# Expert weights of a mixture-of-experts block: 16 KB buffers and runs in place of 8 KB ones

## The chip, the cores and the metric

The kernel runs on one core of a Trainium2 chip. A core has a matrix engine (TensorE, PE in the rows; PEld is its weight load), a vector engine (VectorE, DVE), an activation engine (ScalarE, ACT), GpSimd (POOL) and a sync engine (SyncE, SP), which issues nearly all transfers here. Transfers go from the chip's memory (HBM) to the on-chip memory (SBUF, 128 partitions) by 16 DMA engines. The metric is the time of one execution in device microseconds (us); lower is better.

## The reference, cut to what matters

One transformer block over 256 latent tokens of width 1024 with 256 context tokens. A token mixer (projections, a gated linear recurrence, a spatial MLP, an output projection) is followed by a mixture of 32 experts, of which each token uses 4:

```python
x = x + g1 * token_mix(p_lat, s_fwd, s_bwd, ...)
x = x + g2 * moe_ffn(modulate(x, norm2_g, sh2, sc2), ...)
return rms_norm(x, final_g)

def expert_block(xblk, e):                       # w1: (32, 1024, 2048), w2: (32, 1024, 1024), float32
    z = xblk @ w1[e] + b1[e]
    gate = minimum(z[:, :1024], 7); lin = clip(z[:, 1024:], -7, 7)
    return (gate * sigmoid(1.702 * gate) * (lin + 1)) @ w2[e] + b2[e]
```

Every expert's weights are read once: 8 MB of `w1` and 4 MB of `w2` each, 384 MB in all (1 MB is 1024 KB here). The values stay float32.

## The kernel before

**The mixer.** Its weights come in granules of 256 columns: 1 MB, 128 partitions by 8 rows of 256 values, so that one contiguous run is 1 KB (`Granule`, load at L293). A granule is split into a high and a low part (`ghi` on ScalarE, `glo` on VectorE, L241 and L242), in two halves, and multiplied at L321. After the attention come, in this order: section 6 of `w_in` (4 granules, into `v`), section 5 (4, into `u`, with the small products `o_ps` at L624), `w_branch_b` (4), section 7 and `w_branch_a` (8), `w_out` (4), and then the routing.

**The experts.** `w1_step` (L795 to L800) loads 128 rows of `w1` (1 MB, L797): one row of 2048 values, 8 KB, to a partition, then multiplies 64 gathered tokens by it. Eight such steps make one expert's first product; `swiglu` and `turned` (L818) follow. `w2_steps` (L823 to L839) loads `w2` in four pieces of 1 MB (L832): 16 KB of it belong to a partition, taken in two runs of 8 KB. The second product of an expert comes after the first product of the next one. `scatter` (L855) adds the result to the tokens.

**The end.** For the last expert `last_columns` (L857 to L880) takes `w2` in four blocks of 256 columns, each in two transfers of 512 KB (L863, runs of 1 KB). A block is multiplied (L868), scaled (L871), scattered (L876, L877) and multiplied by the final norm's weight (L880); after the last block come the norm's factor and the output.

**Buffers.** `wtile` (L45) takes the next name from the list `slots`: 8 KB to a partition each. During the attention there are three (`ring`); for the loads after the third granule of section 6 there are seven more (`ringb`, in the space that the attention leaves). For the experts `d0` to `d3`, `big1` (once) and five of `ringc` are added: 20 buffers, 20 MB.

**What sets the order.** A scheduler decides the order on each engine ahead of the run by its own model of the times; in the expert part TensorE keeps the order of the program (`manual_schedule`). Each engine takes its instructions in order. A transfer is issued when its buffer is free and one of eight semaphores that stand for transfers under way is free.

Of the kernel before, what the change touches and what calls it, by code (L numbers as in the profile page):

```python
# [16 lines left out]
P = 128  # L17
# [14 lines left out]
def kernel(  # L32
# [10 lines left out]
    slots = [(ring, "w")] * RING_A  # L43

    def wtile(shape):  # L45

        pool, tag = slots.pop(0)
        if tag != "big1":
            slots.append((pool, tag))
        return pool.tile(shape, F32, name="w", tag=tag)  # L50

# [155 lines left out]
    def mod_col(j, h, res):  # L207
        a, step = mod_sums(j, h)

        def finish():  # L210
            step(1)
            pt = bank("tp", (P, 4, 2))
            for k in range(4):
                te.matmul(pt[:, k], a[:, k * P:(k + 1) * P], ones[:, 0:2], start=True, stop=True)
            ve.tensor_add(res[:, 4 * h:4 * h + 4], pt[:, :, 0], bmcol[:, 8 * j + 4 * h:8 * j + 4 * h + 4])
        return [lambda: step(0), finish]
# [134 lines left out]

    pack2 = pack_rows("pack2", [(rows(norm2_g), 8), (rows(lb_fwd), 16), (rows(lb_bwd), 16), (rows(gnorm_g), 1), (b_s[0], 8)])
    cols2 = unpack(pack2, "cols2")
    n2col, gncol = cols2[:, 0:8], cols2[:, 40:41]
# [179 lines left out]
    for j in range(5):  # L534
# [22 lines left out]
        if j == 0:  # L557
# [11 lines left out]
            nc.sync.dma_start(wr_sb, w_router[0].rearrange("(k p) e -> p k e", p=P))  # L569
# [20 lines left out]
    def more_slots(n):  # L590
        if n == LATER:
            slots.extend([(ringb, "w")] * RING_B)

    more_slots(0)
# [4 lines left out]
    for j in range(4):  # L599
        pp = two(win(6, j), hT[0], True)  # L600
        more_slots(j + 1)
        sc.activation(v[:, :, j * 256:(j + 1) * 256], pp, AF.Gelu)
# [13 lines left out]
    for j in range(4):  # L616
        pp = two(win(5, j), hT[0], False)
        more_slots(j + 5)
# [54 lines left out]
    for j in range(4):  # L673
# [14 lines left out]
        for k in range(2):  # L688
            for tt in range(2):
                te.transpose(pt[:, k, tt * P:(tt + 1) * P], acc[:, tt, (2 * j + k) * P:(2 * j + k + 1) * P], ident)  # L690
# [56 lines left out]
    slots[4:4] = [(consts, f"d{i}") for i in range(4)] + [(consts, "big1")]  # L747
    slots += [(ringc, "w")] * RING_C
# [46 lines left out]
    def w1_step(zz, xT, kt, src):  # L795
        w = wtile([P, 2 * D])
        nc.sync.dma_start(w, src)  # L797
        for n in range(2):
            for h in range(2):
                te.matmul(zz[n][h * C:(h + 1) * C], xT[:, kt], w[:, n * D + h * 512:n * D + (h + 1) * 512],  # L800
# [22 lines left out]
    def w2_steps(hT2, selb, w2e):  # L823
# [6 lines left out]
        for k2 in range(4):  # L830
            w = wtile([P, 2, D])
            nc.sync.dma_start(w, w2e[:, k2 // 2, k2 % 2 * 2:k2 % 2 * 2 + 2])  # L832
# [9 lines left out]
    def scatter(y, pT, wcol, old=None, tts=(0, 1)):  # L842
# [6 lines left out]
        for tt in tts:  # L849
            pcs = [bank2(f"sc{h}") for h in range(2)]  # L850
# [6 lines left out]
    def last_columns(j, hT2, pT, selb, wcol, w2e):  # L857

        selb = selb.to_broadcast([96, C])
        s = slice(j * 256, (j + 1) * 256)  # L860
        w = wtile([P, KT, 256])
        for h in range(2):
            nc.sync.dma_start(w[:, 4 * h:4 * h + 4], w2e[:, h, :, s])  # L863
        py = bank2(("py", "misc")[j % 2], (P, 256))
        te.matmul(py[0:C], selb, b3[:, 2, s], start=True, stop=False, skip_group_check=True)
        for kt in range(KT):
            h = kt % 2
            te.matmul(py[h * C:(h + 1) * C], hT2[:, kt % 4, (kt // 4) * C:(kt // 4) * C + C], w[:, kt],  # L868
                      start=kt == 1, stop=kt >= KT - 2, skip_group_check=True)
        y = wk.tile([P, 256], F32, name="y")  # L870
        ve.tensor_mul(y, py, g2bc[:, s])  # L871

        def rest():
            for tt in range(2):
                pc = bank2((("sc0", "sc1"), ("gate", "lin"))[j % 2][tt], (P, 256))
                te.matmul(pc, pT[:, tt * P:(tt + 1) * P], y, start=True, stop=True)  # L876
                ve.scalar_tensor_tensor(acc[:, tt, s], pc, wcol[tt], acc[:, tt, s], op0=OP.mult, op1=OP.add)  # L877
                junk = wk.tile([P, 256], F32, name="junk", tag="g", bufs=1)
                sc.activation(junk, acc[:, tt, s], AF.Square, accum_out=ss8[:, tt, j:j + 1])
                (gp if j < 3 else ve).tensor_mul(accg[:, tt, s], acc[:, tt, s], fgbc[:, s])  # L880
        return rest
# [21 lines left out]
    w1e = lambda e, kt: w1[0, e, kt * P:(kt + 1) * P]  # L903
# [4 lines left out]
    with tc.manual_schedule(engines={mybir.EngineType.PE}):  # L908
# [3 lines left out]
        for e in range(E):  # L912
# [8 lines left out]
            if e == E - 1:  # L921
                slots[:] = [x for x in slots if x[1] not in ("d0", "d1")]
                bc = consts.tile([P, 2, D], F32, name="bc", tag="d0")
# [3 lines left out]
                ss8 = consts.tile([P, 2, 4], F32, name="ss8")  # L927
            zz = w1_open(sel(e)) if e else first_zz
            for kt in range(KT):
                w1_step(zz, xTs[e], kt, w1e(e, kt))  # L930
# [20 lines left out]
        rest = last_columns(0, hT2, pT, sel(e), wcols(e), w2e(e))  # L951
        scatter(*ready[1:])
        for j in range(1, 4):
            then = last_columns(j, hT2, pT, sel(e), wcols(e), w2e(e))
            rest()
            rest = then
        rest()

    most = nc.values_load(maxc[0:1, 0:1], min_val=0, max_val=T)
    with tc.If(most > C):  # L960
# [5 lines left out]
        with tc.For_i(0, E, 1) as er:  # L966
# [10 lines left out]
            for blk in range(1, T // C):  # L977
# [9 lines left out]
                for kt in range(KT):  # L987
                    w1_step(zz, xT, kt, w1[0, bass.ds(er, 1), kt * P:(kt + 1) * P].rearrange("a p n -> (a p) n"))
# [60 lines left out]
```

## Time and profile before

| | us |
|---|---|
| median of three runs | 1451.89 (1451.4 to 1457.05) |
| the profiled execution | 1452.21 |
| its span, first to last instruction | 1450.4 |
| TensorE busy, share of the span | 93% |
| hardware DMA queue, share of 16 engines' span | 84.3% |

A matrix product counts as busy from when it starts until its modelled end, also where products overlap, so that 93% is not TensorE at its peak. Times within the execution are us from the span's start. "SPq" is the sync engine's issue of a transfer. In a row of the sequence of instructions, rows of one kind are merged (x8 is eight in a row) and the duration is from the first one's start to the last one's end. One float32 product is two matrix instructions in the rows.

### The profile page before, as it was taken

The page shows a single profiled execution, that of the slowest core. Times are in us where ns is not written, and L with a number is a line of the kernel's source. Part 1 is how long each engine was busy: PE and PEld are TensorE (multiplying, and loading weights), DVE is VectorE, ACT ScalarE, POOL GpSimd, SP SyncE. Part 2 cuts the span into 40 slices and gives each one's busy share as a digit, 9 for nine tenths or more (in the row PEclk, how much of TensorE's full clock was granted, in tenths as well). Part 3 has the DMA queues.
Part 4 walks back from the last instruction along what each step waited for, and adds up shares of the span by engine and source line. Part 5 has one row for each costly group of instructions (what it writes and reads, how often), then busy time and mean ns, then how long its engine had stood idle before and what let it go on. Part 6 is the DMA issues. An engine that isn't in the chain of part 4 may idle for free. (4 is left out here: it accounts for less than half of the span.)

```text
span 1450.4 us, 19638 instructions
## 1 busy us (share of the span) xinstructions
PE 1345.7 (93%) x8218; PEld 743.0 (51%) x8218; DVE 640.0 (44%) x1108; ACT 307.9 (21%) x497; POOL 161.1 (11%) x109
## 2 busy tenths in 40 slices
PE   6979798979999999999999999999999999899996
PEld 4979787878999843333333332323323233232323
DVE  5498888887768613222222322222222222222223
ACT  2463354454444310100000000100001000010001
POOL 3054323240064000000000000000000000000001
PEclk8999999999999999999999999999999999999999
DMA  9536252534995899999999999999999999999994
GB/s 333 188 116 204 88 195 67 201 120 162 292 295 220 312 388 414 420 420 421 421 420 420 420 421 420 421 420 421 421 420 421 420 421 422 420 420 421 420 419 173
DMA packets 130751, 487.43 MB, mean 336 GB/s; under 512 B 9161, under 2 KB 71746, under 8 KB 82018
## 3 DMA queue, kind: packets, MB, share of 16 engines
q1 hardware_dynamic: 129810, 483.37, 84.3%
q0 software_dynamic: 848, 2.75, 0.6%
q8 instruction: 66, 1.08, 0.3%
q14 instruction: 27, 0.22, 0.0%
HBM read 485.04 MB, written 1.05 MB: 335 GB/s over the span
## 5 line engine op out<-in xcount | busy, mean ns | idle before, releaser
L800 PE MATMUL gate<-w,xT 128*64 128x512 f32 x1024 | 270.4, 606 | 18.6 <-DMA w<-in_w_dram 17.2
L800 PE MATMUL lin<-w,xT 128*64 128x512 f32 x1024 | 263.5, 592 | 0.0
L836 PE MATMUL py<-w,hT 128*64 128x512 f32 x992 | 228.1, 597 | 20.8 <-DMA w<-in_w_dram 20.8
L321 PE MATMUL acc<-hh,ghi 128*128 128x256 f32 x576 | 166.9, 290 | 12.1 <-ACT iv L394 12.1
L855 DVE SCALAR_TENSOR_TENSOR acc<-sc,wts,acc 128x512 f32<-128x512 f32 x124 | 87.4, 746 | 205.3 <-PE sc L852 205.3
L321 PE MATMUL acc<-hh,glo 128*128 128x256 f32 x576 | 165.5, 288 | 11.3 <-DVE glo L242 11.3
L321 PE MATMUL acc<-hl,ghi 128*128 128x256 f32 x576 | 165.1, 287 | 0.0
L242 DVE TENSOR_TENSOR glo<-w,ghi 128x1024 fp32r<-128x1024 f32 (+1 forms) x99 | 139.1, 1409 | 50.2 <-ACT ghi L241 49.8
L836 PEld LDWEIGHTS py<-w,hT 128*64 128x64 f32 x992 | 66.3, 136 | 162.8 <-issue 98.6
L800 PEld LDWEIGHTS lin<-w,xT 128*64 128x64 f32 x1024 | 74.3, 137 | 145.5 <-issue 145.5
L800 PEld LDWEIGHTS gate<-w,xT 128*64 128x64 f32 x1024 | 61.0, 136 | 163.6 <-issue 96.6
L241 ACT ACTIVATE ghi<-w 128x1024 fp32r<-128x1024 f32 (+1 forms) x102 | 102.4, 1007 | 144.3 <-PE acc L321 106.6
L321 PEld LDWEIGHTS acc<-hh,ghi 128*128 128x128 f32 x576 | 111.4, 194 | 13.3 <-ACT iv L394 12.5
L321 PEld LDWEIGHTS acc<-hh,glo 128*128 128x128 f32 x576 | 111.3, 193 | 13.0 <-DVE glo L242 12.8
L321 PEld LDWEIGHTS acc<-hl,ghi 128*128 128x128 f32 x576 | 111.4, 193 | 0.7 <-issue 0.7
L839 DVE TENSOR_TENSOR y<-py,g2h 128x512 f32<-128x512 f32 x31 | 21.4, 691 | 188.1 <-PE py L836 188.1
L925 POOL DMA_DIRECT2D bc<-in_final_g_dram x1 | 0.6, 557 | 934.3 <-DMA w<-in_w_dram 934.3
L773 ACT ACTIVATE xT<-misc,sh,a 128x128 f32<-128x128 f32 (+1 forms) x68 | 30.7, 451 | 272.4 <-DVE xT L775 272.4
L807 DVE TENSOR_SCALAR g<-gate 128x512 f32<-128x512 f32 x32 | 22.1, 691 | 147.1 <-PE gate L800 147.1
L321 PE MATMUL acc<-ghi,hh 128*128 128x256 f32 x256 | 73.3, 288 | 14.0 <-DVE og L383 6.4
L775 DVE TENSOR_SCALAR xT<-misc,a,sh 128x128 f32<-128x128 f32 (+1 forms) x68 | 27.2, 401 | 131.0 <-PE misc L769 120.5
L808 ACT ACTIVATE s<-g 128x512 f32<-128x512 f32 x32 | 20.2, 630 | 292.5 <-DVE g L807 292.5
(316 smaller groups left out, 1732.4 us busy)
## 6 DMA issues: line engine op xcount, KB each, us to landing
w<-in_w_dram SPq DMA_DIRECT2D x380, 1024.0 KB, 19.8
w<-in_w_in_dram SPq DMA_DIRECT2D x33, 1024.0 KB, 5.6
w<-in_w_mod_dram SPq DMA_DIRECT2D x24, 1024.0 KB, 6.6
w<-in_w_branch_a_dram SPq DMA_DIRECT2D x4, 1024.0 KB, 16.2
w<-in_w_branch_b_dram SPq DMA_DIRECT2D x4, 1024.0 KB, 12.2
w<-in_w_out_dram SPq DMA_DIRECT2D x4, 1024.0 KB
w<-in_w_dram SPq DMA_DIRECT2D x8, 512.0 KB, 8.7
w<-in_w_in_dram SPq DMA_DIRECT2D x12, 256.0 KB, 7.5
```

The costliest lines, as they stand in the source:

```text
L241: sc.activation(hi, src, AF.Copy)
L242: eng.tensor_sub(lo, src, hi)
L321: te.matmul(o, l, r, start=opens and kt == 0 and n == 0, stop=kt == KT - 1 and n == 2, skip_group_check=True)
L773: sc.activation(xT[:, kt], pg[:, k], AF.Identity, bias=sh2[:, kt:kt + 1], scale=a2[:, kt:kt + 1])
L775: ve.tensor_scalar(xT[:, kt], pg[:, k], a2[:, kt:kt + 1], sh2[:, kt:kt + 1], op0=OP.mult, op1=OP.add)
L800: te.matmul(zz[n][h * C:(h + 1) * C], xT[:, kt], w[:, n * D + h * 512:n * D + (h + 1) * 512], start=False, stop=kt == KT - 1, skip_group_c ...
L807: ve.tensor_scalar(g, zz[0], 7.0, None, op0=OP.min)
L808: sc.activation(s, g, AF.Sigmoid, scale=1.702)
L836: te.matmul(py[h * C:(h + 1) * C], hT2[:, kt % 4, (kt // 4) * C:(kt // 4) * C + C], w[:, k, h * 512:(h + 1) * 512], start=False, stop=kt = ...
L839: ve.tensor_mul(y, py, g2h)
L855: ve.scalar_tensor_tensor(acc[:, tt, s], pcs[h], wcol[tt], old[:, tt, s], op0=OP.mult, op1=OP.add)
L925: gp.dma_start(fgbc, bcast(final_g, D))
```

## The change

- Buffers have a size of one unit (8 KB to a partition) or two (16 KB). `ringb` is three buffers of two units (was seven of one) and `ringc` three of two (was five of one); `ring`, `d0` to `d3` and `big1` stay. That is 20 MB as before. `ringb` no longer serves the mixer, which keeps the three of `ring` to its end.
- `two_units` loads two units of expert weights: into a buffer of two units with one transfer of 2 MB and runs of 16 KB, or, where the next buffer is of one unit, with two transfers of 1 MB and runs of 8 KB. For that a partition holds two neighbouring rows of `w1`; the order of the tokens' columns follows (`cols3`, `view(..., [[2, P]])`, the router's weights in four transfers, three small loads `pack3`).
- The last expert's `w2` comes in four transfers of 1 MB (`last_columns`): half the rows by 512 columns, runs of 2 KB. The last half is multiplied in two blocks of 256 columns. The `scatter` before it uses four PSUM banks in place of two.
- In the expert part SyncE keeps the order of the program too.

```diff
-    slots = [(ring, "w")] * RING_A
+    slots = [(ring, "w", 1)] * RING_A
+    def wtile(shape, units=1):
+        i = next(i for i, s in enumerate(slots) if s[2] == units)
+        pool, tag, _ = slots.pop(i)
+        if tag != "big1":
+            slots.append((pool, tag, units))
+        return pool.tile(shape, F32, name="w", tag=tag)
+    def two_units(src, n):
+        r = 4096 // n
+        if slots[0][2] == 2:
+            w = wtile([P, r, n], 2)
+            nc.sync.dma_start(w, src)
+            return w[:, :r // 2], w[:, r // 2:]
+        ws = [wtile([P, r // 2, n]) for _ in range(2)]
+        for i, w in enumerate(ws):
+            nc.sync.dma_start(w, src[:, i * (r // 2):(i + 1) * (r // 2)])
+        return ws
...
-                te.matmul(pt[:, k], a[:, k * P:(k + 1) * P], ones[:, 0:2], start=True, stop=True)
+                te.matmul(pt[:, k], view(a, k // 2 * 256 + k % 2, [[2, P]]), ones[:, 0:2], start=True, stop=True)
...
+    pack3 = late.tile([12, 256], F32, name="pack3")
+    for i, src in enumerate((norm2_g[0], b_mod[0, 3 * D:4 * D], b_mod[0, 4 * D:5 * D])):
+        nc.sync.dma_start(pack3[4 * i:4 * i + 4], src.rearrange("(r f) -> r f", f=256))
...
-            nc.sync.dma_start(wr_sb, w_router[0].rearrange("(k p) e -> p k e", p=P))
+            for r in range(4):
+                nc.sync.dma_start(wr_sb[:, 2 * r:2 * r + 2], w_router[0, r * 256:r * 256 + 256].rearrange("(p k) e -> p k e", k=2))
...
-    def more_slots(n):
-        if n == LATER:
-            slots.extend([(ringb, "w")] * RING_B)
...
-    slots[4:4] = [(consts, f"d{i}") for i in range(4)] + [(consts, "big1")]
-    slots += [(ringc, "w")] * RING_C
+    slots[:] = ([(ringb, "w", 2)] * RING_B + slots + [(consts, f"d{i}", 1) for i in range(4)] + [(consts, "big1", 1)] +
+                [(ringc, "w", 2)] * RING_C)
...
-                    te.matmul(pg[:, k], x1[:, tt, kt * P:(kt + 1) * P], tok[:, tt], start=tt == 0, stop=tt == 1)
+                    te.matmul(pg[:, k], view(x1, tt * D + kt // 2 * 256 + kt % 2, [[2, P]]), tok[:, tt], start=tt == 0, stop=tt == 1)
...
-    def last_columns(j, hT2, pT, selb, wcol, w2e):
+    def last_columns(c, hT2, pT, selb, wcol, w2e):
...
+        def products(u):
...
+            w = wtile([P, 4, 512])
+            nc.sync.dma_start(w, w2e[:, u, :, c * 512:(c + 1) * 512])
+            for b in blocks if u else [slice(0, 512)]:
...
-    with tc.manual_schedule(engines={mybir.EngineType.PE}):
+    with tc.manual_schedule(engines={mybir.EngineType.PE, mybir.EngineType.SP}):
...
+        first, last = (last_columns(c, hT2, pT, sel(e), wcols(e), w2e(e)) for c in range(2))
+        first[0]()
+        scatter(*ready[1:], banks=("sc0", "sc1", "gate", "lin"))
+        first[1]()
+        last[0]()
+        first[2]()
+        last[1]()
+        last[2]()
...
-RING_B = 7
-RING_C = 5
+RING_B = 3
+RING_C = 3
```

What the sync engine issues from the last loads of the attention part on, before (128x8x256 is a mixer granule of 1 MB, x6 is six of them; `in_w_dram` is an expert weight):

```order
L188 DMA w<-in_w_mod_dram 128x4x512
L293 DMA w<-in_w_in_dram 128x8x256 x6
L293 DMA w<-in_w_branch_a_dram 128x8x256
L293 DMA w<-in_w_in_dram 128x8x256 x2
L293 DMA w<-in_w_branch_b_dram 128x8x256 x4
```

And now, at the same place of the same engine:

```order
L201 DMA w<-in_w_mod_dram 128x4x512
L306 DMA w<-in_w_in_dram 128x8x256 x7
L58 DMA w<-in_w_dram 128x4096 x3
L306 DMA w<-in_w_in_dram 128x8x256
L306 DMA w<-in_w_branch_b_dram 128x8x256 x4
```

Three expert transfers of 2 MB have moved ahead of the last granule of section 5. At the end of the mixer the same engine had, before (the eight and four are one expert's `w1` and `w2`; `maxc` is the read of the largest expert's count):

```order
L293 DMA w<-in_w_out_dram 128x8x256 x4
L797 DMA w<-in_w_dram 128x2048 x16
L832 DMA w<-in_w_dram 128x2048 x4
L959 TENSOR_LOAD maxc
L959 ISA x2
L797 DMA w<-in_w_dram 128x2048 x8
```

And now:

```order
L306 DMA w<-in_w_out_dram 128x8x256 x4
L62 DMA w<-in_w_dram 128x2048 x8
L58 DMA w<-in_w_dram 128x4096 x3
L986 TENSOR_LOAD maxc
L986 ISA x2
L58 DMA w<-in_w_dram 128x4096 x3
L62 DMA w<-in_w_dram 128x2048 x8
L58 DMA w<-in_w_dram 128x4096 x6
```

From there eight transfers of 1 MB and six of 2 MB alternate to the end: 114 of 2 MB in all, 152 of 1 MB and the last four. The order of the expert weights was that of their use before as well.

TensorE's order where the last granule of section 5 begins, before (`acc_4127` is the third granule's result, `acc_4198` the last one's; the small products of the third and fourth part of `u` stood inside and behind the last granule):

```order
L321 MATMUL acc_4127<-hl0_169,ghi_4156 128x256
L321 MATMUL acc_4127<-hh0_168,glo_4157 128x256
L321 MATMUL acc_4198<-hh0_168,ghi_4199 128x256
L321 MATMUL acc_4198<-hl0_169,ghi_4199 128x256
L321 MATMUL acc_4198<-hh0_168,glo_4200 128x256
```

And now, at the same place (`o_ps` is the small products, `ub` a part of the router's offset, `acc_4210` the last granule's result):

```order
L334 MATMUL acc_4139<-hh0_168,glo_4169 128x256
L671 MATMUL ub_4550<-wr_sb_61,sh2_71 128x32 x3
L640 MATMUL o_ps_4198<-wsT_987,v_3725 128x128 x4
L640 MATMUL o_ps_4269<-wsT_987,v_3725 128x128 x4
L334 MATMUL acc_4210<-hh0_168,ghi_4211 128x256
```

Small products that don't need the last granule now stand ahead of it. TensorE's order in the last expert's last columns, before:

```order
L865 LDWEIGHTS sel_69
L865 MATMUL misc<-b_4507,sel_69 64x256
L868 MATMUL misc<-w,hT_9605 64x256 x8
L876 MATMUL sc_9707<-y,pT 128x256
L876 MATMUL sc_9713<-y,pT 128x256
L876 MATMUL gate<-y,pT 128x256
L876 MATMUL lin<-y,pT 128x256
```

And now:

```order
L882 LDWEIGHTS sel_69
L882 MATMUL misc<-b_4519,sel_69 64x512
L888 MATMUL misc<-w,hT_9389 64x512 x4
L899 MATMUL sc_9432<-y,pT 128x512
L899 MATMUL sc_9438<-y,pT 128x512
L888 MATMUL misc<-w,hT_9389 64x256 x8
L899 MATMUL gate<-y,pT 128x256
L899 MATMUL lin<-y,pT 128x256
L899 MATMUL sc_9468<-y,pT 128x256
L899 MATMUL sc_9474<-y,pT 128x256
```

The four blocks of 256 columns have become one of 512 and two of 256, over the same columns and rows in all.

## Rows read from the trace of the kernel before

**Rows 1.** Stretches: us, busy us of PE PEld DVE ACT POOL, clock, DMA share, GB/s.

```profile
380.00:410.00 30.00, 30.00 (x258) 30.00 (x257) 21.00 (x34) 13.09 (x17) 3.50 (x6) 1.00 1.09 344
436.00:510.00 74.00, 72.92 (x597) 68.21 (x598) 51.78 (x91) 31.66 (x51) 16.31 (x11) 1.00 0.72 274
510.00:560.00 50.00, 47.88 (x255) 20.56 (x251) 10.82 (x26) 7.18 (x13) 0.00 (x0) 1.00 0.98 391
560.00:1400.00 840.00, 802.26 (x3795) 279.09 (x3791) 223.32 (x396) 61.19 (x114) 0.56 (x1) 1.00 1.01 421
1421.00:1428.00 7.00, 5.94 (x34) 2.47 (x34) 2.38 (x5) 0.60 (x1) 0.00 (x0) 1.00 1.02 337
```

**Rows 2.** What SyncE's issues waited for: us in total, times, longest.

```profile
SPq L797 <- DMA w<-in_w_dram: 435.3, 209, 3.6
SPq L832 <- DMA w<-in_w_dram: 220.6, 105, 3.6
SPq L797 <- PE lin L800: 44.6, 39, 3.6
```

**Rows 3.** Issues of expert loads in order of time, SyncE: start, us, instruction.

```profile
541.81 16.26 SPq L797 DMA_DIRECT2D w<-in_w_dram  x8
...
568.75 14.13 SPq L797 DMA_DIRECT2D w<-in_w_dram  x8
...
1379.79 10.25 SPq L797 DMA_DIRECT2D w<-in_w_dram  x5
```

**Rows 4.** The DMA view: instruction loads' packets, expert loads with KB and median landing.

```profile
q8 instruction: 66, 1.08, 0.3%
...
w<-in_w_dram SPq DMA_DIRECT2D x380, 1024.0 KB, 19.8
```

**Rows 5.** Issues of loads by SyncE in order of time, mixer and its end.

```profile
368.65 0.37 SPq L293 DMA_DIRECT2D w<-in_w_branch_a_dram  x1
...
442.34 54.18 SPq L797 DMA_DIRECT2D w<-in_w_dram  x15
500.77 2.08 SPq L832 DMA_DIRECT2D w<-in_w_dram  x4
```

**Rows 6.** Line L797 in 380 to 560 us: time from issue to landing.

```profile
DMA to landing us min/median/max: 4.8/8.2/10.1
```

**Rows 7.** VectorE in order of time: the splits' low halves, the attention's last write.

```profile
370.84 0.42 DVE L242 TENSOR_TENSOR ylo<-y,yhi 128x256 fp32r<-128x256 f32 x1
372.81 1.23 DVE L242 TENSOR_TENSOR glo<-w,ghi 128x1024 fp32r<-128x1024 f32 x1 [1.55 <-ACT ghi L241]
```

**Rows 8.** TensorE in order of time: the small products of section 5.

```profile
391.63 1.05 PE L624 MATMUL o_ps<-wsT,v 128*128 128x128 f32 x8
```

**Rows 9.** Waits of the whole run: ScalarE's split and TensorE's products for weights.

```profile
ACT ghi L241 <- DMA w<-in_w_in_dram: 6.2, 4, 3.1
...
PEld py L836 <- DMA w<-in_w_dram: 62.7, 55, 1.9
```

**Rows 10.** TensorE in order of time, end of the experts.

```profile
1420.88 1.94 PE L836 MATMUL py<-w,hT 128*64 128x512 f32 x8 [0.62 <-DMA w<-in_w_dram]
...
1424.18 1.95 PE L868 MATMUL py<-w,hT 128*64 128x256 f32 x16 [0.25 <-ACT hT L820]
...
1428.02 1.78 PE L852 MATMUL sc<-y,pT 64*128 64x512 f32 x4 [0.84 <-DVE acc L855]
...
1439.12 0.59 PE L876 MATMUL lin<-y,pT 128*128 128x256 f32 x2
```

**Rows 11.** Weight loads of transposes: 4-apart and contiguous; us, mean ns before the bar.

```profile
L818 PEld LDWEIGHTS misc<-ident,l 128*128 128x128 f32 x128 | 17.9, 209 | 28.1 <-issue 25.1 <-DVE l L811 3.0
...
L690 PEld LDWEIGHTS tp<-ident,acc 128*128 128x128 f32 x16 | 1.9, 145 | 0.2 <-DVE acc L686 0.2
```

**Rows 12.** SyncE in order of time: the last small load and the next weights.

```profile
44.63 0.43 SPq L569 DMA_DIRECT2D wr_sb<-in_w_router_dram  x1
57.77 7.79 SPq L293 DMA_DIRECT2D w<-in_w_in_dram  x3
```

More of the change, by code (lines that the diff above doesn't have):

```diff
@@ L840, in w2_steps, with scatter @@
         return y
-    def scatter(y, pT, wcol, old=None, tts=(0, 1)):
+    def scatter(y, pT, wcol, old=None, tts=(0, 1), banks=("sc0", "sc1") * 2):
         nonlocal acc
@@ L849, in scatter @@
         for tt in tts:
-            pcs = [bank2(f"sc{h}") for h in range(2)]
+            pcs = [bank2(banks[2 * tt + h]) for h in range(2)]
             for h in range(2):
@@ L855, in scatter @@
                 ve.scalar_tensor_tensor(acc[:, tt, s], pcs[h], wcol[tt], old[:, tt, s], op0=OP.mult, op1=OP.add)
-    def last_columns(j, hT2, pT, selb, wcol, w2e):
+    def last_columns(c, hT2, pT, selb, wcol, w2e):
         selb = selb.to_broadcast([96, C])
[L860 to L871, printed above, removed]
-        def rest():
[L874 to L881, printed above, removed]
@@ new lines, in last_columns @@
+        py = bank2(("py", "misc")[c])
+        y = wk.tile([P, 512], F32, name="y")
+        blocks = [slice(0, 512)] if c == 0 else [slice(0, 256), slice(256, 512)]
+        def products(u):
+            if u == 0:
+                te.matmul(py[0:C], selb, b3[:, 2, c * 512:(c + 1) * 512], start=True, stop=False, skip_group_check=True)
+            w = wtile([P, 4, 512])
+            nc.sync.dma_start(w, w2e[:, u, :, c * 512:(c + 1) * 512])
+            for b in blocks if u else [slice(0, 512)]:
+                for k in range(4):
+                    h = k % 2
+                    te.matmul(py[h * C:(h + 1) * C, b], hT2[:, k, u * C:u * C + C], w[:, k, b],
+                              start=u == 0 and k == 1, stop=u == 1 and k >= 2, skip_group_check=True)
+                if u:
+                    ve.tensor_mul(y[:, b], py[:, b], g2bc[:, c * 512 + b.start:c * 512 + b.stop])
@@ new lines, in rest @@
+        def rest():
+            for i, b in enumerate(blocks):
+                n = b.stop - b.start
+                s = slice(c * 512 + b.start, c * 512 + b.stop)
+                for tt in range(2):
+                    pc = bank2((("sc0", "sc1"), ("gate", "lin"))[(c + i) % 2][tt], (P, n))
+                    te.matmul(pc, pT[:, tt * P:(tt + 1) * P], y[:, b], start=True, stop=True)
+                    ve.scalar_tensor_tensor(acc[:, tt, s], pc, wcol[tt], acc[:, tt, s], op0=OP.mult, op1=OP.add)
+                    junk = wk.tile([P, n], F32, name="junk", tag="g", bufs=1)
+                    sc.activation(junk, acc[:, tt, s], AF.Square, accum_out=ss8[:, tt, c + i:c + i + 1])
+                    (ve if i else gp).tensor_mul(accg[:, tt, s], acc[:, tt, s], fgbc[:, s])
@@ L883 @@
+        return [lambda: products(0), lambda: products(1), rest]
     tok, xTs = {}, {}
@@ L922 @@
                 slots[:] = [x for x in slots if x[1] not in ("d0", "d1")]
+                assert slots[0][2] == 2 or sum(x[2] == 1 for x in slots) >= 2
                 bc = consts.tile([P, 2, D], F32, name="bc", tag="d0")
@@ L950 @@
         pT = spread(identb[:, e:e + 1], 0)
[L951 to L957, printed above, removed]
+        first, last = (last_columns(c, hT2, pT, sel(e), wcols(e), w2e(e)) for c in range(2))
[6 more added lines that the diff above has]
+        last[2]()
     most = nc.values_load(maxc[0:1, 0:1], min_val=0, max_val=T)
@@ L992 @@
         for tt in range(2):
-            for j in range(4):
-                s = slice(j * 256, (j + 1) * 256)
-                junk = wk.tile([P, 256], F32, name="junk", tag="g", bufs=1)
+            for j, s in enumerate((slice(0, 512), slice(512, 768), slice(768, 1024))):
+                junk = wk.tile([P, s.stop - s.start], F32, name="junk", tag="g", bufs=1)
                 sc.activation(junk, acc[:, tt, s], AF.Square, accum_out=ss8[:, tt, j:j + 1])
@@ L1014 @@
 FIRST = 6
-LATER = 3
 MOD_POOL = (0,)
```

41 lines of the change are left out of this document (22 added, 19 removed).

## The prediction

> **What bounds the kernel now.** I read the stretches first [rows 1]. From 560 to 1400 us the DMA engines are busy all the time (share 1.01) and move 421 GB/s; that is 840 of the span's 1450.4 us with nothing to vary it. TensorE's 802 us of 840 look as high, so the second look is at who waits for whom. SyncE, which issues the weights, waits 435.3 and 220.6 us for transfers to land before it may issue the next, and 44.6 us for the matrix products of L800 to free a buffer [rows 2]: transfers are the scarce thing, buffers are not. TensorE waits for weights 55 times at L836, up to 1.9 us [rows 9]. Third, the two paces. While buffers are still full, early in the experts, issues follow TensorE: one expert's first load comes at 541.81 and the next one's at 568.75 us, 26.94 us for 12 MB [rows 3]. Late, they follow the DMA: five issues in 10.25 us, so (10.25 - 0.33)/4 = 2.48 us for 1 MB, 29.8 us an expert. The experts are bound by transfers, and TensorE could go 2.8 us an expert faster.
>
> Ahead of that, TensorE is the bound: it is busy for 30.00 of 30 us at 380 to 410 and for 72.92 of 74 at 436 to 510 [rows 1]. From 510 to 560 the DMA moves 391 GB/s since all 20 MB are full at times. Behind it, from about 1421 us, the last expert's chain runs on TensorE and VectorE [rows 10].
>
> **The change part by part.**
>
> *Runs of 16 KB.* The cost of a run's start shows in stretches of full DMA with different runs. Where all loads have runs of 1 KB the engines move 344 and 337 GB/s, with 8 KB 421 [rows 1]. On one of 16 engines a 1 KB run therefore takes 1024 x 16/344 = 47.6 ns (48.6 by 337), an 8 KB run 8192 x 16/421 = 311.3. If a run costs a + b x bytes, a = (8 x 47.6 - 311.3)/7 = 9.9 ns (11.1 by the other). A transfer of 2 MB has 128 runs of 16 KB, 8 on each engine, in place of 16: it saves 8 x 9.9 = 79 ns (89). Of the 114 such transfers three lie in the mixer, where the DMA has time; 111 count: 111 x 79 = 8.8 us, 9.8 at most, and I take **-9.0**. The lower end is no gain at all, as no run of 16 KB shows on this queue; the only ones in the trace are 66 instruction loads, 0.3% of 16 engines' span [rows 4], which is 0.003 x 16 x 1450.4/66 = 1.05 us each, taken beside weight packets. That is far over 2 x 311 ns, but they shared the engine; I give it little weight.
>
> By the Trainium skill ("DMA: Bandwidth & Descriptors", Why small descriptors are slow) a packet costs a fixed three cycles or so inside the engine and each operation 32 bytes of metadata on the fabric. With the page's 32 bytes a cycle at 850 MHz that is four cycles, 4.7 ns, and the term an estimated 111 x 8 x 4.7 = 4.2 us, less than half of mine. The rows' intercept of 10 ns speaks against it, though it comes from 1 KB runs.
>
> *Where the transfers begin.* Three transfers of 2 MB now stand ahead of section 5's last granule. Their buffers lie where the attention was, whose last write ends at 370.84 + 0.42 = 371.26 us [rows 7]; SyncE has issued the granule before at 368.65 [rows 5]. A load alone takes 4.8 us [rows 6], 2.3 before and after 2.5 of transfer. So the 6 MB occupy the DMA from about 373.9 (behind the granule issued at 368.65) to 388.6 us, and the last granule, whose buffer is free when the split at 372.81 ends (374.04 [rows 7]), takes 3.0 us of 1 KB runs behind them: 391.6. Its first split is two steps of about 1.2 us (the second is 1.23 [rows 7]): 394.0. Before, TensorE reached the last granule at 393.2: the small products at 391.63 [rows 8] take 0.8 and six products at 0.116 (30.00 us for 258 [rows 1]) follow. Now two groups of small products at 0.8 stand ahead of it, the `ub` products and a wait for VectorE between the groups, together some 1 us by my estimate: 395 to 396. No stall, by a margin of 1 us. After it each granule is one load of 4.9 us in a ring of three, against 48 x 0.116 = 5.6 us of products; a ring of three served the attention too, and ScalarE waited for `w_in` four times in the run, 6.2 us in all [rows 9]. I take **+0.5**, from 0 to +5.
>
> At the mixer's end eight transfers of 1 MB wait in order for the last three granules' buffers; before, 15 were spread over 54.18 us by such waits and the last four went at 500.77 [rows 5], to land within 13 us. Now some 6 MB are left when the third buffer comes free at about 487, then 6 MB of `ringc` at 496 to 501: by my estimate the 20 MB are in at 519, 5 us later, but TensorE needs the last of them only at 547. From there the DMA has no gap, where before it paused (274 and 391 GB/s [rows 1]). Followed load by load at 2.48 us, 42 MB have landed at about 573.5 us against 574.3: **-0.8**, from -3 to +2; a buffer of 2 MB, held until both halves are used, eats the rest.
>
> *The last expert.* Four loads of 1 MB with 2 KB runs come faster than eight of 1 KB, but TensorE's chain sets the end. Before: the last `w2` piece's products of the expert ahead begin at 1420.88 and the last products end at 1439.7 [rows 10], 18.8 us. Now that `w2` piece is 2 MB, so 3.9 us of products follow its landing in place of 1.94; 1.36 to the first columns' product; four products at 2.0 (1.95 at 1424.18), two scatters at 1.1 without the 0.84 wait, two rests at 1.1, and 0.8 of the last block's scaling: 18.5, with the final norm's part after it as before. **0**, from -3 to +3.
>
> *At no cost.* Six more small loads are 3 to 4 us of SyncE's time, in the gap between its last small load at 44.63 and the next weights at 57.77 [rows 12], which wait for a buffer; without the gap they would cost those 4 us. Weight loads of every second value: those of every fourth take 209 ns where contiguous ones take 145 [rows 11], so up to 64 ns for some 48 ahead of the experts, **+0.5**, from 0 to 3; the others hide in TensorE's 2.8 us an expert. The order of the expert loads was that of their use before; holding it changes nothing.
>
> *Sum.* -9.0 + 0.5 - 0.8 + 0 + 0.5 = -8.8 us. The profiled execution took 1452.21 (span 1450.4), 0.3 over the median of 1451.89, so 1443.4 in its terms and about **1443.2** as a median.
>
> **The rivals.**
> 1. *A run's start costs half.* If part of the 10 ns overlaps with data in long runs, the term is -4.4 us and the time 1447.7. For it: the shares over 1 [rows 1], packets that overlap. The skill's three cycles and 32 bytes are this case.
> 2. *The size gains nothing.* The engines are fed by a queue that lands 19.8 us after its issue [rows 4], so neither fewer issues nor larger transfers matter, and at 8 KB the limit may be the memory. Then only the small terms stay: 1452. The skill's rule (same page, Rules for kernel authors: at least 1 MiB and 128 partitions for full bandwidth) is met by the old transfers, and read so promises nothing. Against it, 344 against 421 GB/s.
> 3. *Slower: the ring of three starves the mixer.* Place: the 17 granules from section 5's last one on, TensorE being the bound there. Price: the mean of ScalarE's waits, 6.2/4 = 1.55 us, at each granule is 26 us, with the gain of 9 a time of 1469. It decides from 16.3 us of stalls, 0.96 a granule, where slower by 0.5% begins. Against it, 4.9 us of load for 5.7 of products.
> 4. *More gain:* the slowest engine profits most, or the pauses at 510 to 560 go altogether: -14 us, 1438.
>
> **How the numbers follow.** About 0.5%, 7.3 us, is what a measurement of this kernel can tell from no change. Forecast 0.58 (1440.5 to 1446), half 0.15, nothing 0.15, slower 0.06, more 0.06. The forecast's own spread puts two thirds of it under 1444.6: faster 0.38 + 0.06 and a little of rival 1, 0.48; slower 0.06; same 0.46. The range of 8 in 10 goes from 1439 to 1453: it leaves out rivals 3 and 4 and the edges of the forecast and of rival 2.
>
> **What would show it.** GB/s at 600 to 1400 us: about 425 (421 if rival 2, 423 if rival 1), as 111 of the stretch's transfers are only part of it. Packets of 16 KB about twice 311 less 10 ns. TensorE busy without a gap at 390 to 400 us and at 410 to 500, its first L800-like product within 2 us of 508. A last product near 1431. Wrong, if TensorE waits in the mixer, if packets of 16 KB take over 622 ns, or if the DMA pauses after 520.

## The result and the profile after

The changed kernel takes 1476.40 us (median of four runs, 1471.32 to 1479.67) against 1452.49 beside it: a ratio of 1.0155, 95% interval 1.0118 to 1.0193. It is slower by 23.9 us, where 1443.2 with a range of 1439 to 1453 was predicted. The profiled execution took 1477.94 us, its span is 1476.1.

In the changed kernel L814 and L851 are the products of `w1` and `w2` (L800 and L836 before), and L334 is the mixer's.

The stretches of the changed kernel, as in [rows 1] (stretch, length, busy us of each engine, granted clock of TensorE, DMA share, GB/s):

```profile
380.00:410.00 30.00, 28.27 (x238) 27.88 (x238) 21.79 (x34) 12.83 (x16) 10.68 (x9) 1.00 0.95 338
436.00:510.00 74.00, 73.17 (x598) 70.02 (x597) 49.66 (x82) 32.50 (x50) 10.89 (x6) 1.00 0.66 234
510.00:560.00 50.00, 47.88 (x239) 23.71 (x240) 12.37 (x36) 8.21 (x16) 0.00 (x0) 0.90 0.92 387
560.00:600.00 40.00, 40.00 (x187) 12.82 (x183) 10.23 (x16) 1.82 (x3) 0.00 (x0) 1.00 0.46 191
600.00:1400.00 800.00, 751.11 (x3555) 268.88 (x3553) 208.70 (x374) 58.76 (x110) 0.00 (x0) 1.00 1.01 424
```

The last row is the gain that was hoped for: 424 GB/s where [rows 1] has 421. The row above it is most of the loss. Between 560 and 600 us the DMA engines are busy for less than half the time. The line of GB/s in 40 slices shows that this happens once (16th number) and never again:

```profile
GB/s 334 183 110 202 92 193 89 169 142 145 342 206 197 323 419 123 424 425 426 423 423 426 425 424 421 427 423 423 423 427 423 423 424 426 424 421 425 427 422 184
```

What stops the transfers is in SyncE's queue. First its waits over the whole run (total us, times, longest; L58 loads 2 MB, L62 loads 1 MB, L884 the last four loads), then its issues in order of time (start, us from the first one's start to the last one's end, number):

```profile
SPq L62 <- DMA w<-in_w_dram: 580.6, 135, 12.0
SPq L62 <- PE lin L814: 109.0, 27, 30.0
SPq L58 <- DMA w<-in_w_dram: 82.5, 46, 2.3
SPq L884 <- PE misc L796: 13.7, 1, 13.7
```

```profile
541.25 39.89 SPq L62 DMA_DIRECT2D w<-in_w_dram  x6
581.18 2.78 SPq L58 DMA_DIRECT2D w<-in_w_dram  x5
```

The fifth of those six 1 MB loads is issued at 550.34, the sixth at 580.81: SyncE stands for 30 us on TensorE's products, and as soon as it may go on it issues five loads of 2 MB within 2.78 us. Their buffers came free during the wait: in e10_order_not_held below, where these loads may pass the one that waits, the first of them goes at 561.69. In [rows 2] the longest wait for those products was 3.6 us.

Why one load waits so long is in the list of buffers. `big1` is taken once and leaves the list, so that after the first cycle seven one-unit buffers are left, while pairs always take two. The fourth pair of a cycle takes the seventh one and then the next one-unit buffer of the list: the one that was loaded first in this same cycle. Walked through from the code of the diff, with the MB loaded between two loads of one buffer:

```
changed kernel    18 MB: 227 times    19: 7    10: 4    6: 17    4: 1
e1_even_pairs     30: 18    18: 93    16: 117    19 or 24 or 31: 8    12 to 14: 7
```

At 550 us the buffers are full, so the load that has to be used up first lies some 30 us of TensorE's work ahead.

### The profile page after: what moved, and what is told of

It reads as the page before. It is cut to its first block, busy times and chain, and to the rows that moved or that the text cites. A ratio compares the mean times of both kernels' runs of the same rounds, so it can differ in the third digit from the quotient of the medians.

```text
span 1476.1 us, 19217 instructions
## 1 busy us (share of the span) xinstructions
PE 1356.6 (92%) x8190; PEld 755.2 (51%) x8190; DVE 639.5 (43%) x1106; ACT 307.8 (21%) x493; POOL 160.1 (11%) x107
## 5 line engine op out<-in xcount | busy, mean ns | idle before, releaser
L814 PE MATMUL gate<-w,xT 128*64 128x512 f32 x1024 | 272.4, 611 | 25.6 <-DMA w<-in_w_dram 24.8
L814 PE MATMUL lin<-w,xT 128*64 128x512 f32 x1024 | 265.0, 596 | 0.0
L851 PE MATMUL py<-w,hT 128*64 128x512 f32 x992 | 225.6, 599 | 30.0 <-DMA w<-in_w_dram 30.0
L334 PE MATMUL acc<-hh,ghi 128*128 128x256 f32 x576 | 167.9, 292 | 11.4 <-ACT iv L416 11.4
L334 PE MATMUL acc<-hh,glo 128*128 128x256 f32 x576 | 166.3, 289 | 10.6 <-DVE glo L255 10.6
L334 PE MATMUL acc<-hl,ghi 128*128 128x256 f32 x576 | 165.9, 288 | 1.4 <-DVE hl L255 1.4
L851 PEld LDWEIGHTS py<-w,hT 128*64 128x64 f32 x992 | 70.0, 137 | 166.0 <-issue 109.3
L814 PEld LDWEIGHTS lin<-w,xT 128*64 128x64 f32 x1024 | 73.9, 138 | 148.4 <-issue 148.4
L814 PEld LDWEIGHTS gate<-w,xT 128*64 128x64 f32 x1024 | 62.0, 137 | 169.8 <-issue 93.3
L334 PEld LDWEIGHTS acc<-hh,ghi 128*128 128x128 f32 x576 | 111.9, 194 | 12.7 <-ACT iv L416 11.8
L334 PEld LDWEIGHTS acc<-hh,glo 128*128 128x128 f32 x576 | 111.7, 194 | 12.2 <-DVE glo L255 11.9
L334 PEld LDWEIGHTS acc<-hl,ghi 128*128 128x128 f32 x576 | 111.9, 194 | 2.2 <-DVE hl L255 1.6
L334 PE MATMUL acc<-ghi,hh 128*128 128x256 f32 x256 | 73.7, 290 | 12.4 <-DVE og L405 6.3
L785 PEld LDWEIGHTS misc<-p,acc 128*128 128x128 f32 x544 | 68.6, 201 | 26.6 <-issue 26.0
```

Source lines behind the costliest of these rows:

```text
L334: te.matmul(o, l, r, start=opens and kt == 0 and n == 0, stop=kt == KT - 1 and n == 2, skip_group_check=True)
L785: te.matmul(pg[:, k], view(x1, tt * D + kt // 2 * 256 + kt % 2, [[2, P]]), tok[:, tt], start=tt == 0, stop=tt == 1)
L814: te.matmul(zz[n][h * C:(h + 1) * C], xT[:, kt], w[:, 0, n * D + h * 512:n * D + (h + 1) * 512], start=False, stop=kt == KT - 1, skip_grou ...
```

## The experiments

Each kernel's times stand against runs of the kernel before on the same chip. A cycle is one pass through the list of buffers.

### Is it the odd buffer?

**e1_even_pairs.** Two one-unit buffers make a pair only when both are next in the list.

```diff
-        if slots[0][2] == 2:
+        if slots[0][2] == 2 or slots[1][2] == 2:
```

> The changed kernel, but two one-unit buffers are taken as a pair only when both stand at the head of the list; one alone waits there and the next two-unit buffer is taken ahead of it. So no buffer is loaded twice within one cycle of the list. Theory A (the same-cycle re-use of the odd buffer stops SyncE at 550 us for 30 us and throws away the 20 MB that lie ahead): the 40 us stretch after the first expert moves over 380 GB/s in place of 191, some 21 us come back, and 3 to 6 more at the end, where the last four loads find a buffer earlier: 1448 to 1455. Rival B (the ring of three in the mixer, the later start of the experts and the end make the loss; what is lost at 560 us is made up for later since TensorE could go 2.8 us an expert faster): at most 5 us come back, 1470 to 1476.

1453.69 us against 1451.54, ratio 1.0011 (0.999 to 1.0032). Of the 23.9 us, 21.8 are gone. The stretch at 560 is full, and the wait of 30 us has gone: the longest for those products is 6.0 us (stretches, then SyncE's waits for products of L814, of e1_even_pairs):

```profile
560.00:600.00 40.00, 40.00 (x191) 13.76 (x186) 10.22 (x16) 2.25 (x5) 0.00 (x0) 1.00 1.01 422
600.00:1400.00 800.00, 761.28 (x3616) 272.38 (x3615) 211.49 (x378) 59.08 (x110) 0.56 (x1) 1.00 1.01 425
```

```profile
SPq L58 <- PE lin L814: 74.8, 18, 6.0
SPq L62 <- PE lin L814: 31.3, 17, 4.7
```

**e2_six_singles.** The same by another way: one buffer less, so that three whole pairs are left.

```diff
-        if tag != "big1":
+        if tag not in ("big1", "d3"):
             slots.append((pool, tag, units))
```

> The changed kernel, but d3 is given up with big1 after its first use: six one-unit buffers, three whole pairs, 18 MB in place of 19, the rule for pairs as in the changed kernel. Theory A (an odd number of one-unit buffers is the cause, not the room): 1449 to 1457, in spite of 1 MB less. Rival B (the mixer and the end): 1470 to 1478. Rival C (the room ahead is what counts): slower than the changed kernel.

1454.35 us, ratio 1.0011 (0.999 to 1.0033). A buffer less is 21 us faster than the odd one. It is the re-use, not the room.

**e3_oldest_for_tail.** The last four loads take the oldest buffer of any size.

```diff
-            w = wtile([P, 4, 512])
+            w = wtile([P, 4, 512], slots[0][2])
```

> The changed kernel, but the last expert's four loads take whichever buffer is the oldest in the list, three of them two-unit buffers of which they fill half. If the end is late because these loads wait for one of five one-unit buffers (one is held 13.7 us), the last load lands some 10 us earlier than at 1457, and the time is 1464 to 1471; if the end follows from the pause at 560 us alone, it stays at 1473 to 1478.

1475.6 us, ratio 1.0148 (1.0115 to 1.0181). The wait of 13.7 us at L884 is gone (the longest of that line is now 2.6 us), the last load lands at 1455.28 in place of 1457.03, and nothing clear of the noise is gained in the time. The end is late because all that lies ahead of it is late.

### One re-use in the kernel before

If the reason is right, it must work in the kernel before as well. There, ahead of one expert, the buffer that was loaded six loads earlier is put at the head of the list, once:

```diff
+            if e == 3:
+                slots.insert(0, slots.pop(-6))
             zz = w1_open(sel(e)) if e else first_zz
```

**e8_one_early_reuse** is this, **e9_one_late_reuse** the same with `e == 20`, **e12_before_held** the kernel before with SyncE held to the program's order (`manual_schedule` for PE and SP), **e11_early_reuse_held** e8 and e12 together.

> The kernel before with one thing changed once: ahead of the fourth expert's first load (issued at 541.81 us before) the list's head becomes the buffer that was loaded six loads earlier; everything after goes in the new order, oldest first. Theory A (one same-cycle re-use while buffers are full makes SyncE wait until TensorE has come through what lies ahead, and the DMA runs empty): a wait of 20 to 30 us, 15 to 24 us slower than before, 1466 to 1476. Rival B (the stock is made up for, or SyncE's order is not the point): within 4 us of before.

> The same single step ahead of the 21st expert's first load, at about 1095 us, where TensorE waits for weights and some eight transfers are under way. Theory A (the re-use costs only the stock that it throws away, and here there is none): SyncE waits some 10 us more once, five loads are still under way, and the time is that of before within 3 us, 1450 to 1455. If each such wait costs its own length, 10 us or more: 1461 and up.

> e8_one_early_reuse with SyncE's transfers held to the order of the program: the re-used buffer's load stands where the program has it, seven others behind it. Theory A: SyncE waits some 20 to 30 us near 542, the DMA runs empty, and the time is 10 to 22 us over the kernel before: 1461 to 1473. Rival B (a single re-use is made up for): 1449 to 1454, as without the hold.

> The kernel before with SyncE's transfers held to the order of the program in the expert part, and nothing else: the loads stand in the order of their use there already, so every theory gives the time of before within 3 us, 1449 to 1454. It is the measure for e11_early_reuse_held. If holding the order costs by itself, 1455 or more.

| kernel | us | before | ratio (95%) |
|---|---|---|---|
| e8_one_early_reuse | 1451.01 | 1451.61 | 0.9998 (0.9985 to 1.0011) |
| e12_before_held | 1451.62 | 1452.23 | 1.0001 (0.9985 to 1.0016) |
| e11_early_reuse_held | 1475.31 | 1452.23 | 1.0168 (1.0154 to 1.0182) |
| e9_one_late_reuse | 1451.23 | 1451.61 | 1.0002 (0.9982 to 1.0022) |

e8 was a miss: I had not thought of the scheduler. SyncE is not held there, and the scheduler put the load that must wait behind eleven others. SyncE's issues in e8_one_early_reuse:

```profile
540.24 13.31 SPq L797 DMA_DIRECT2D w<-in_w_dram  x7
556.17 7.89 SPq L832 DMA_DIRECT2D w<-in_w_dram  x4
565.45 0.33 SPq L797 DMA_DIRECT2D w<-in_w_dram  x1
```

The first row should have eight loads; the eighth is the one at 565.45. TensorE waited 2.3 us for it, once. With the order held, in e11_early_reuse_held, the same single step stops everything (issues, then SyncE's waits at 535 to 572 us, then the stretches):

```profile
533.84 4.17 SPq L832 DMA_DIRECT2D w<-in_w_dram  x2
568.05 4.14 SPq L797 DMA_DIRECT2D w<-in_w_dram  x8
```

```profile
SPq L797 <- PE lin L800: 29.9, 1, 29.9
```

```profile
510.00:560.00 50.00, 47.88 (x253) 20.31 (x251) 12.24 (x28) 7.20 (x13) 0.00 (x0) 1.00 0.64 257
560.00:600.00 40.00, 40.00 (x198) 15.08 (x200) 12.17 (x24) 3.69 (x7) 0.00 (x0) 1.00 0.77 320
```

That is more than the 10 to 22 us that were expected. One wait of 29.9 us leaves the DMA idle for 0.36 of 50 and 0.23 of 40 us, 27 us, and costs 23 us in the end. Little of it comes back in 800 us, since the rest is bound by transfers: some 11 MB that TensorE had in hand (27 us at 421 GB/s) were used up without being replaced.

e9 shows the other side. SyncE is not held there either, and as in e8 the load that must wait goes behind eleven others (seven of L797 from 1041.23 us, four of L832 from 1058.63), so it is not SyncE that waits, as was expected. TensorE waits 14.26 us for the re-used buffer, and the time is unchanged: while it waits the transfers go on at 420 GB/s, and TensorE is faster than they are (timeline of TensorE, then the stretch of the wait):

```profile
1076.04 1.97 PE L800 MATMUL gate<-w,xT 128*64 128x512 f32 x4 [14.26 <-DMA w<-in_w_dram]
```

```profile
1062.00:1076.00 14.00, 0.00 (x0) 0.00 (x0) 0.00 (x0) 0.00 (x0) 0.00 (x0) 0.63 1.01 420
```

So idle time of the DMA counts nearly in full, one late wait of TensorE not at all. A late re-use with the order held was not run by itself; the changed kernel has 16 of them after 6 MB behind the first one, and moves 424 GB/s there.

### Is the held order the fault?

**e10_order_not_held** is the changed kernel with `manual_schedule` for PE alone.

> The changed kernel with one part undone: SyncE's transfers are not held to the order of the program; the scheduler may move them. In its order the load that re-uses the odd buffer goes behind the six 2 MB loads that stood behind it. Theory A (what costs is the held order together with the re-use: six free buffers wait behind one that is not): no wait of 30 us, over 380 GB/s at 560 to 600 us, 1449 to 1457. Rival B (the re-use costs in either order, since TensorE needs that load next anyway): 1468 to 1478.

1472.54 us, ratio 1.0149 (1.0129 to 1.0169): rival B held, theory A fell. The scheduler lets six loads of 2 MB pass the load that waits, and the DMA has no long pause (issues, then stretches of e10_order_not_held):

```profile
561.69 21.70 SPq L58 DMA_DIRECT2D w<-in_w_dram  x6
584.77 0.33 SPq L62 DMA_DIRECT2D w<-in_w_dram  x1
```

```profile
560.00:600.00 40.00, 39.35 (x186) 12.71 (x182) 10.34 (x16) 2.57 (x5) 0.00 (x0) 1.00 0.94 389
600.00:1400.00 800.00, 749.57 (x3539) 272.46 (x3537) 208.84 (x374) 58.74 (x110) 0.00 (x0) 0.97 1.01 424
1400.00:1430.00 30.00, 30.00 (x139) 9.51 (x137) 7.33 (x12) 1.23 (x3) 0.56 (x1) 1.00 0.83 335
```

But now the load comes behind six others of 2 MB that TensorE needs later, and it comes so in every cycle. TensorE's waits in that kernel, and SyncE's longest in total:

```profile
PE gate L814 <- DMA w<-in_w_dram: 40.4, 11, 6.1
PE py L851 <- DMA w<-in_w_dram: 10.7, 6, 3.3
```

```profile
SPq L58 <- PE lin L814: 266.9, 56, 8.7
```

17 waits, some 50 us apart, 51.1 us in all; the list has 17 re-uses after 6 MB. TensorE is now the late one: in the last row it is busy for all of its 30 us while the transfers fall to 335 GB/s, and SyncE waits for its products, where in the changed kernel it waits for transfers (580.6 us at L62).

The waits alone are not the whole cost. e1's profiled execution has 40.3 us of such waits too, in 49, so that e10 waits 10.8 us more, and is 26.8 us longer (1478.68 against 1451.92). Its experts begin 7.3 us later (518.76 against 511.45), and TensorE's granted clock is 0.97 in the long stretch against 1.00: it falls to the lower of its two levels, 1.2 GHz, at nine of the 17 waits, the longest among them. How the rest divides was not tried. In the changed kernel the re-use costs the stock once; here it costs TensorE a little each time. The odd buffer is the fault in either order (e13 below, neither held nor with an early re-use, takes 1450.78 us), and the hold only decides who pays. e8 against e11 is the case where that matters.

### Where the gain of the runs goes

e1 is free of the fault and still no faster than before. Six kernels take it apart.

**e5_all_8KB:** the changed kernel, each two-unit buffer as two of one unit (`RING_B = RING_C = 6`).

> The changed kernel with each of its six two-unit buffers as two one-unit ones: every load 1 MB with runs of 8 KB, the order of the uses oldest first, so no re-use within a cycle either. Against e1_even_pairs this differs in the length of the runs and the size of the transfers alone. If 16 KB runs bring 12 ns for two (616 against 2 x 314 ns in the changed kernel's packets), it is 9 to 11 us slower than e1_even_pairs: 1457 to 1466. If the size of the runs brings nothing, the two are equal within 3 us.

**e4_mixer_on_three:** the kernel before, with `ringb` given to the experts' first loads in place of the mixer, and six buffers of one unit each in `ringb` and `ringc`.

```diff
-    slots[4:4] = [(consts, f"d{i}") for i in range(4)] + [(consts, "big1")]
-    slots += [(ringc, "w")] * RING_C
+    slots[:] = ([(ringb, "w")] * RING_B + slots + [(consts, f"d{i}") for i in range(4)] + [(consts, "big1")] +
+                [(ringc, "w")] * RING_C)
...
-LATER = 3
+LATER = 99
...
-RING_B = 7
-RING_C = 5
+RING_B = 6
+RING_C = 6
```

> The kernel before with one part of the change alone: ringb and ringc are six one-unit buffers each, and ringb no longer serves the mixer but takes the experts' first six loads. All loads are those of the kernel before (1 MB, 8 KB runs, the old end). Theory A (the mixer with three buffers costs what the 16 KB runs bring, since 3 MB less have been moved by 580 us in e1_even_pairs than before): 5 to 8 us slower than before, 1456 to 1460. Rival B (that loss is due to buffers of 2 MB, held until both halves are used, or to the weight loads of every second value): 1450 to 1454.

**e7_halves_in_mixer:** e1, and `ringb` serves the mixer, two granules to a buffer (the edit in `wtile`; the list starts in another order too). **e13_halves_not_held:** the same, SyncE not held.

```diff
+        if units == 1 and (halves or (shape[1] == KT and slots[0][2] == 2)):
+            if not halves:
+                slots.append(slots.pop(0))
+                pair = ringb.tile([P, 2, KT, 256], F32, name="w", tag="w")
+                halves.extend([pair[:, 0], pair[:, 1]])
+            return halves.pop(0)
...
```

> e1_even_pairs, and ringb serves the mixer again from the third granule of section 6 on, as before: a two-unit buffer there holds two granules, one in each half. Theory A (the ring of three is the cost that is left): TensorE has no gap at 380 to 410 us, the first turned is back at about 528 to 530 in place of 531.9, and the time is 1444 to 1449, 4 to 8 us under e1_even_pairs. Rival B (it is the buffers of 2 MB, or the strided weight loads): within 3 us of e1_even_pairs, 1451 to 1456.

> e7_halves_in_mixer (pairs whole, ringb in halves in the mixer) with SyncE's order not held. Theory A (what 16 KB runs bring is lost where buffers of 2 MB come free late, at 510 to 560 us, and an order that goes round waiting loads saves part of it): 1 to 4 us under e7_halves_in_mixer, 1446 to 1449. If the order no longer matters once no buffer is re-used early, within 1 us of it: 1449 to 1451.

**e14_singles_rest_after:** the changed kernel with the one-unit buffers of before. **e15_halves_8KB_runs:** e7, a two-unit buffer filled by two transfers of 1 MB.

> The changed kernel with the buffers of before: all of one unit, ringb in the mixer, 8 KB runs; of the change stay the order of rows in a partition (weight loads of every second value, small loads), the last expert's four blocks and the held order. Theory A (the change's other parts cost nothing, and the gain of the 16 KB runs goes where buffers of 2 MB come free): the time of before within 3 us, 1449 to 1455. Rival B (the strided weight loads or the end cost what the runs bring): 1456 to 1460.

> e7_halves_in_mixer with the same buffers in the same order, but a two-unit buffer of the experts is filled by two transfers of 1 MB with runs of 8 KB. It differs from e7_halves_in_mixer in the runs alone, and from e14_singles_rest_after in the buffers alone. Theory A: 6 to 9 us over e7_halves_in_mixer, 1456 to 1460, the price of buffers of 2 MB where no run pays for it. Rival B (smaller transfers start and land earlier, and the runs bring little): 1449 to 1453.

| kernel | us | before | ratio (95%) |
|---|---|---|---|
| e4_mixer_on_three | 1454.72 | 1451.61 | 1.0030 (1.0010 to 1.0050) |
| e5_all_8KB | 1460.72 | 1451.54 | 1.0063 (1.0043 to 1.0083) |
| e14_singles_rest_after | 1454.83 | 1452.68 | 1.0019 (1.0001 to 1.0036) |
| e15_halves_8KB_runs | 1459.56 | 1452.68 | 1.0046 (1.0023 to 1.0069) |
| e7_halves_in_mixer | 1450.40 | 1451.61 | 0.9993 (0.9976 to 1.0010) |
| e13_halves_not_held | 1450.78 | 1452.23 | 0.9994 (0.9982 to 1.0007) |

e4 and e7 came out between the ranges of their two theories, so neither theory held as it was put; e13 is where the order no longer matters.

In differences from before, each step against the one above it:

| step | kernels | us |
|---|---|---|
| rows, small loads, strided weight loads, end, hold | e14 | +2.2 |
| buffers of 2 MB | e15 less e14 | +4.7 |
| runs of 16 KB | e7 less e15 | -8.1 |
| the mixer on a ring of three | e1 less e7 | +3.4 |
| the odd buffer | changed less e1 | +21.8 |
| sum, before rounding | changed kernel | +23.9 |

Each of the small terms is uncertain by some 3 to 4 us, by the two intervals that go into it, so that the mixer's is not clear of nothing by itself; e4, on its own (+3.1, interval 1.5 to 7.3 us), confirms it. The step from e14 to e15 has nine granule buffers in the mixer in place of ten as well. e5 is the one that fits badly: it lacks the buffers of 2 MB as well as the runs, so that by the table it should be 3.4 us over e1 (-4.7 + 8.1), and it is 7.0; that is within the intervals, no more.

The traces say the same in another unit. Two stretches of each kernel, 410 to 560 us (the buffers fill) and 560 to 1400 us; the rows are, in this order, of e14, e15, e7, e1 and the changed kernel:

```profile
410.00:560.00 150.00, 147.17 (x1059) 115.46 (x1058) 82.78 (x129) 50.15 (x75) 36.29 (x23) 1.00 0.82 309
560.00:1400.00 840.00, 803.07 (x3787) 281.45 (x3787) 221.99 (x394) 61.20 (x114) 0.56 (x1) 1.00 1.01 420
```

```profile
410.00:560.00 150.00, 146.74 (x1062) 116.21 (x1062) 85.43 (x130) 51.15 (x76) 37.08 (x23) 1.00 0.80 300
560.00:1400.00 840.00, 800.69 (x3769) 279.67 (x3766) 221.46 (x394) 60.64 (x113) 0.56 (x1) 1.00 1.01 420
```

```profile
410.00:560.00 150.00, 146.00 (x1050) 114.57 (x1049) 82.62 (x129) 49.27 (x75) 34.12 (x22) 1.00 0.80 300
560.00:1400.00 840.00, 797.29 (x3801) 289.15 (x3799) 223.24 (x396) 61.23 (x114) 0.56 (x1) 1.00 1.01 425
```

```profile
410.00:560.00 150.00, 145.76 (x1059) 116.52 (x1059) 80.95 (x131) 50.46 (x76) 28.16 (x20) 1.00 0.78 291
560.00:1400.00 840.00, 801.28 (x3805) 286.14 (x3799) 221.71 (x394) 61.33 (x115) 0.56 (x1) 1.00 1.01 424
```

```profile
410.00:560.00 150.00, 145.70 (x1039) 118.17 (x1039) 81.24 (x131) 50.75 (x75) 29.70 (x20) 0.97 0.75 280
560.00:1400.00 840.00, 791.11 (x3740) 281.70 (x3736) 218.93 (x390) 60.58 (x113) 0.00 (x0) 1.00 0.98 413
```

The last column is to be read as bytes missing. From e14 to e15 (buffers of 2 MB) the filling falls from 309 to 300 GB/s: 9 x 150 = 1.35 MB less, 3.2 us at 421 GB/s, beside +4.7 measured. From e7 to e1 (mixer on three) another 9 GB/s, 3.2 us, beside +3.4. From e15 to e7 (runs) the long stretch rises from 420 to 425: 5 x 840 = 4.2 MB, 10 us by rounded figures, beside -8.1. From e1 to the changed kernel it falls by 11: 9.2 MB, 21.9 us, and the filling by 11, 3.9 us; their profiled executions differ by 26.0 (1477.94 and 1451.92).

e7 differs from e15 in the size of its transfers too, 2 MB against 1 MB. What the runs do by themselves shows in the trace of the changed kernel, which has both in one stretch: from 600 to 1400 us a packet of 16 KB took 617.3 ns in mean (12513 packets), one of 8 KB 314.7 ns (16390). One run start less saves 2 x 314.7 - 617.3 = 12.1 ns.

So the gain of the runs is real, and where the list is sound it is spent on filling the buffers later. e7 and e13 are the best kernels here: 1.6% faster than the changed one, and not to be told from the one before. e13 shows that once no buffer is re-used early the hold makes no difference.

## Why the prediction was wrong

**What bounds the kernel** held: transfers, TensorE with time to spare in the experts.

**Runs of 16 KB** (-9.0): held. -8.1 measured, for 111 transfers and 8 runs saved on each engine 9.1 ns a run, where the rows of 1 KB runs gave 9.9, and the packets themselves show 12.1. By the Trainium skill ("DMA: Bandwidth & Descriptors", Why small descriptors are slow) it is three cycles and 32 bytes, from which an estimate of 4.2 us was made. That lies at the edge of what the two intervals allow; 8.1 us in the times, 420 against 425 GB/s and the 12.1 ns in the traces speak for the rows of this case.

**Where the transfers begin** is the step that failed. "From there the DMA has no gap" and the -0.8 us rest on following the loads one by one with buffers that come free in the order of the list. I followed them through the first cycle, where there are eight one-unit buffers and all pairs are whole. The second cycle begins near 520 us, with seven. The sections ahead of the prediction had both facts, `big1` "once" and pairs of two, and the prediction did not put them together. In place of a DMA without a gap the trace has a share of 0.46 from 560 to 600 us, behind one wait of SyncE of 30.0 us. The term was +21.8 us in place of -0.8, and its mark, "if the DMA pauses after 520", is what the trace shows. The part that was only mis-sized is "a buffer of 2 MB, held until both halves are used, eats the rest": +4.7 us, where the whole term was to lie between -3 and +2.

**"The order of the expert loads was that of their use before; holding it changes nothing"** is right for the kernel before (e12) and for e13, and wrong beside a re-use: e8 and e11 differ by the hold alone, by 24 us. That it is at fault in the changed kernel, as I then thought, fell with e10.

**The mixer on three** (+0.5, from 0 to +5): +3.1 to +3.4. The margin of 1 us at the last granule of section 5 wasn't there. TensorE waits three times, 3.1 us in all, with the same waits in e4 (TensorE's waits at 390 to 416 us, changed kernel):

```profile
PE acc L334 <- DVE hl L255: 1.4, 1, 1.4
PE acc L334 <- DVE glo L255: 0.9, 1, 0.9
PE o_ps L640 <- DVE t L643: 0.8, 1, 0.8
```

The rival that was to be slower (TensorE starved at 17 granules, 26 us) named a stretch that has such waits at its start alone: from 416 to 510 us none is over 0.3 us. Its price was eight times too high, and the kernel is slower for another reason.

**The last expert** (0, from -3 to +3): no difference seen. In e1 the last 2 MB piece's products begin at 1420.42 and the last product ends at 1439.6, 19.2 us, where 18.5 were worked out and [rows 10] has 18.8.

**The small loads and the strided weight loads** (0 and +0.5): with the end and the hold +2.2, interval 0.1 to 5.2 us; what of it is which wasn't tried.

**The marks.** 424 GB/s came (about 425 was given), and packets of 16 KB at 617.3 ns, under the 622 that would have been wrong. The mixer's gaps showed that step wrong; the first product of the experts, due within 2 us of 508, began at 515.04, and the last product, due near 1431, ended at 1465.5.

## What to carry to other kernels

Where buffers of several sizes share one list, walk through it for a few cycles and write down the bytes between two loads of each buffer: the smallest number counts, not the mean, and the cycle after one-time buffers have left is the one to look at. Where a stretch bound by transfers follows one in which buffers fill, read the GB/s of the filling as bytes in hand: what is missing there is paid at the rate of the long stretch, and a wait of the faster engine is not while it can catch up (e9; in e10 it no longer could). A larger transfer has to earn back the coarser release of its buffer.

## What the hardware showed that I had not expected

The cost of a run's start is about as large between 8 and 16 KB (9.1 ns from the times, uncertain by nearly half; 12.1 from the packets) as between 1 and 8 KB (9.9): no sign that long runs hide it.

The profiled execution of the changed kernel started its experts later than the gaps in the mixer explain. TensorE's granted clock there, in stretches of 5 us:

```profile
505.00:510.00 5.00, 4.30 (x29) 2.42 (x28) 4.39 (x26) 0.40 (x2) 0.00 (x0) 1.00 1.04 433
510.00:515.00 5.00, 5.00 (x26) 4.93 (x25) 1.69 (x9) 0.81 (x2) 0.00 (x0) 0.53 1.01 428
515.00:520.00 5.00, 5.00 (x21) 1.63 (x22) 0.69 (x2) 0.81 (x2) 0.00 (x0) 0.79 1.03 436
520.00:525.00 5.00, 5.00 (x32) 2.74 (x28) 0.00 (x0) 0.00 (x0) 0.00 (x0) 1.00 0.99 423
```

A mean of 0.53 is nearly all at 1.2 GHz, the lower of its two levels; it came after 0.70 us of idle time in the routing, and the 32 products of the gathering took 6.08 us. In e1 the same stretch has the same 4.30 us of busy time, the clock stays at 1.00, and they take 3.98 us (from 507.54). The profiled execution of e10 has it too (0.50 from 515 to 520 us). What made the difference stays open; it is some 4 us of the changed kernel's profiled execution, which is 26.0 us longer than e1's where the medians differ by 21.8.
